# A 128-byte unused tile ahead of the constants of a one-layer decoder kernel

## The chip, the cores and the metric

The kernel runs on one core of a Trainium2 chip. The metric is the time of one execution on the device in microseconds, as the median of several runs; lower is better.

## What is computed

One layer of a decoder trunk on x of 1024 rows by 1024 columns, all in float32:

```python
x = x + 0.5 * swiglu(rms_norm(x, g_ffn1), w1_gate, w1_up, w1_down)      # D_FF = 2816
h = rms_norm(x, g_mix)
proj = h @ w_in                                                         # queries, keys, values, gates
y_a = dsa_attention(...)             # indexer, top 256 keys of each row, softmax, 8 heads
y_b = stick_breaking_attention(...)  # strictly causal, no softmax, 8 heads
merged = sigmoid(gate_a) * (y_a @ w_o_a) + sigmoid(gate_b) * (y_b @ w_o_b)
x = x + merged @ w_out
x = x + 0.5 * swiglu(rms_norm(x, g_ffn2), w2_gate, w2_up, w2_down)
```

## The kernel before

**Products.** A float32 operand is held as two halves, the part that fits TensorE's fast float32 form ("hi") and the rest ("lo"), and a product is three matmuls into one PSUM bank: hi by hi, hi by lo, lo by hi. `mm3` (L304 to L306) does this for the projections, `times` (L463 to L465) for the gate and up products of the two feed-forward blocks, and L672 to L674 for their down products. Both feed-forward blocks use Strassen's scheme: seven products of quarter matrices in place of eight, so sums and differences of quarters (S1 to S4 of the weights, T1 to T4 of the rows) are made first.

A matmul has a stationary operand (128 by 128, which the weight load puts into the array) and a moving one (here mostly 128 by 512, which streams through it). In float32 the moving one covers 2048 bytes of each partition and the stationary one 512 bytes.

```python
def times(a, b, ps, start=True):                                     # L460
    for k in range(4):
        c, l = slice(k * P, (k + 1) * P), slice(512 + k * P, 512 + (k + 1) * P)
        nc.tensor.matmul(ps, a[:, c], b[k][:, HI], ...)              # L463: a stationary, b moving
        nc.tensor.matmul(ps, a[:, c], b[k][:, LO], ...)              # L464
        nc.tensor.matmul(ps, a[:, l], b[k][:, HI], ...)              # L465
```

So a product of `times` is 12 matmuls. The products of one block stand in the order S1·T1 (bank pd), S2·T2 (pb), S3·T3 (pc), A12·B21 (pa), A22·T4 (pc), S4·B22 (pd), after A11·B11 (pa).

**Where tiles lie.** SBUF is handed out by pools from two ends. Pools of the left side stand behind the constants and small tiles, each behind the one opened before it; pools of the right side stand from the far end of SBUF downwards. The stationary operands of the feed-forward blocks come from `op`, which hands out tiles of two pools in turn:

```python
def ring(pool):                                                      # L737; NR = 5
    op = in_turn((wt, 4), (lambda name: pool.tile([P, 1024], F32R, tag="r", name=name, bufs=NR), NR))
```

`wt` is of the pool `outer` (right, 4 tiles), the other is `ring1` or `ring2` (left, 5 tiles), and `in_turn` (L308) takes them as right, left, right, left, right, left, right, left, left, and again. The moving operands of the gate and up products (B.., T..) lie in `t1` or `t2` (right); those of the down products come from `op` too.

**Places.** Nearly all tiles are a multiple of 512 bytes long, so a pool's tiles all begin at one place within 512 bytes. In the built program of the kernel before, tiles of left pools begin 352 bytes past a multiple of 512, and tiles of right pools 480 past one. "Place" below is this remainder; two tiles are "together" where it is the same, and "apart" where it is not. Exceptions are the small tiles and the weights of the index stage (tag `wM`, 4224 bytes, right side), whose places go on by 128 from tile to tile.

**Order.** In the feed-forward blocks the program's order is a schedule made at build time, in the attention stage one that the class `Weave` writes out from its own table of costs. Neither looks at addresses.

Of the kernel before, what the change touches and what calls it, by code (L numbers as in the profile page):

```python
# [10 lines left out]
F32 = mybir.dt.float32  # L11
# [12 lines left out]
P = 128  # L24
# [220 lines left out]
def trunk(ctx, tc, x, positions, g_ffn1, w1_gate, w1_up, w1_down, g_mix, w_in, g_cq, w_uq_a, w_q_idx,  # L245
          g_q_a, g_k_a, w_uv_a, w_o_a, w_o_b, w_out, g_ffn2, w2_gate, w2_up, w2_down, inv_freq, out):
    nc = tc.nc
    cst = ctx.enter_context(tc.tile_pool(name="cst", bufs=1))
# [16 lines left out]
        return small.tile([P, n], dt, name=name, bufs=bufs)  # L265


    ident = cst.tile([P, P], F32, name="ident")
    make_identity(nc, ident)
    mhalf = cst.tile([P, H], F32, name="mhalf")  # L270
# [1836 lines left out]
```

## Time and profile before

| | us |
|---|---|
| median of 3 runs | 2323.19 (2322.38 to 2325.25) |
| the profiled execution, own time | 2324.09 |
| its span from first to last instruction | 2322.3 |
| of that TensorE busy | 2211.2 (95%) |
| VectorE, ScalarE, GpSimd busy | 1590.9, 1114.3, 881.6 |

The stages in time: up to 342 us gate and up products of the first block with their opening, to 690 its down products, to 760 the first projections, to 1506 attention with the rest of the projections woven in, to 1640 the output projections, to 1980 the second block's gate and up products, to the end its down products (the lines run over these bounds a little). Matmuls follow each other faster than one takes from start to end, so what a matmul costs is read from one start to the next, not from its duration.

### The profile page before, as it was taken

To read this page: it belongs to the slowest core of one execution; us is meant where nothing else is said; L and a number is where in the kernel's file an instruction comes from. 1 tells how busy PE (TensorE), PEld (TensorE's weight loads), DVE (VectorE), ACT (ScalarE), POOL (GpSimd) and SP (SyncE) were. 2 spreads that over 40 slices of the span, in tenths; PEclk is the share of its full clock that TensorE was granted. 3 is DMA by queue.
4 is the path that set the end of the run, shared out by engine and by line. 5 is a ranking of instruction groups with operands and counts; after the bars stand their busy time and mean duration, and the time that the engine had idled before them with its cause. 6 is when DMAs were issued, how large, how long until landed. Compare 5 with 4: busy or idle time off the path is not lost.

```text
span 2322.3 us, 30186 instructions
## 1 busy us (share of the span) xinstructions
PE 2211.2 (95%) x10460; PEld 1811.4 (78%) x10460; DVE 1590.9 (69%) x2512; ACT 1114.3 (48%) x2133; POOL 881.6 (38%) x648
## 2 busy tenths in 40 slices
PE   7999999999999898889999699999999999999999
PEld 6788888878879777667788578877878888888877
DVE  5765656678862897666698877862476565667685
ACT  4323232334452479889988456633342323233443
POOL 3555555432252444211122133146245555542233
PEclk9999999999999999999999799999999999999999
DMA  5232323587664243645454533357313333358755
GB/s 165 75 114 91 114 87 116 159 307 241 168 208 116 81 132 98 163 98 128 109 138 120 172 109 97 128 178 254 118 59 109 96 107 98 105 163 291 234 168 181
DMA packets 252538, 330.64 MB, mean 142 GB/s; under 512 B 20577, under 2 KB 155377, under 8 KB 252385
## 3 DMA queue, kind: packets, MB, share of 16 engines
q1 hardware_dynamic: 235264, 288.83, 41.4%
q0 software_dynamic: 7488, 24.16, 2.7%
q10 hardware_dynamic: 9632, 15.73, 2.0%
q8 instruction: 82, 1.34, 0.2%
q14 instruction: 72, 0.58, 0.1%
HBM read 234.78 MB, written 93.88 MB: 142 GB/s over the span
## 4 chain that ended last, share of the span: by engine, by line
PE 70%; DVE 11%; ACT 9%; DMA 4%; issue 4%; POOL 1%; ACTq 0%; SPq 0%; DVEq 0%; POOLq 0%
PE p L673 5%; PE p L674 5%; PE p L672 5%; ACT junka L1127 4%; PE pc L463 3%; PE pc L465 3%; PE pc L464 3%; PE pd L465 3%; PE pd L463 3%; PE pd L464 3%; PE pa L463 3%; PE pa L465 3%; PE pa L464 3%; PE pb L463 2%; PE pb L465 2%
## 5 line engine op out<-in xcount | busy, mean ns | idle before, releaser
L1127 ACT ACTIVATE junka<-u,cand,sig 128x1024 bf16<-128x1024 f32 (+5 forms) x186 | 182.7, 982 | 22.1 <-DVE cand L1124 10.0
L1563 DVE TENSOR_TENSOR_SCAN left<-left 128x640 f32<-128x640 f32 (+3 forms) x64 | 92.7, 1449 | 3.8 <-ACT left L1555 3.8
L1612 DVE TENSOR_TENSOR pt<-pstT,pt 128x512 fp32r<-128x512 f32 (+1 forms) x96 | 51.3, 551 | 22.0 <-ACT pt L1610 21.4
L1664 PE MATMUL pstT<-ident,sa 128*128 128x128 f32 x288 | 47.4, 279 | 13.7 <-DVE pt L1612 12.0
L1729 DVE CUSTOM_DVE_ANT_0 e<-psL,bias 128x512 f32<-128x512 f32 (+3 forms) x96 | 49.4, 549 | 14.4 <-PE psL L1766 14.4
L1612 DVE TENSOR_TENSOR pt<-pspT,pt 128x512 fp32r<-128x512 f32 x72 | 46.5, 683 | 18.2 <-ACT pt L1610 18.2
L1741 ACT ACTIVATE e<-e,nm 128x256 f32<-128x256 f32 (+7 forms) x64 | 49.4, 774 | 18.5 <-DVE nm L1736 17.3
L1820 PE MATMUL pspT<-ident,e 128*128 128x128 f32 x288 | 42.0, 285 | 16.2 <-DVE ri L1743 9.2
L1566 DVE TENSOR_TENSOR sa<-sa,left 128x639 f32<-128x639 f32 (+3 forms) x64 | 53.1, 829 | 5.0 <-ACT sa L1557 1.8
L1664 PEld LDWEIGHTS pstT<-ident,sa 128*128 128x128 f32 x288 | 35.1, 142 | 26.2 <-DVE pt L1612 17.5
L673 PE MATMUL p<-bT,bS 128*128 128x512 f32 x132 | 51.8, 392 | 2.7 <-DVE bT L374 2.7
L1631 POOL DMA_DIRECT2D ybld<-yl x16 | 8.8, 551 | 118.8 <-DVE yl L1629 66.3
L1610 ACT ACTIVATE pt<-pspT 128x512 fp32r<-128x512 f32 x72 | 39.5, 596 | 29.8 <-PE pspT L1820 29.5
L673 PE MATMUL p<-aT,aS 128*128 128x512 f32 x132 | 51.8, 393 | 1.1 <-DVE aT L374 1.1
L1820 PEld LDWEIGHTS pspT<-ident,e 128*128 128x128 f32 x288 | 35.3, 146 | 22.5 <-DVE e L1744 9.5
L674 PE MATMUL p<-bT,bS 128*128 128x512 f32 x132 | 51.5, 393 | 0.8 <-POOL bS L374 0.8
L1610 ACT ACTIVATE pt<-pstT 128x512 fp32r<-128x512 f32 (+1 forms) x96 | 46.7, 501 | 11.6 <-PE pstT L1664 10.0
L1476 DVE SCALAR_TENSOR_TENSOR u<-relu,WI,u 128x512 f32<-128x512 f32 (+1 forms) x70 | 49.5, 727 | 3.9 <-ACT relu L1469 2.7
L674 PE MATMUL p<-aT,aS 128*128 128x512 f32 x132 | 50.9, 393 | 0.0
L1557 ACT ACTIVATE sa<-psz 128x512 f32<-128x512 f32 (+2 forms) x96 | 47.0, 503 | 5.0 <-ACT evg L1060 2.4
L1555 ACT ACTIVATE left<-psz 128x512 f32<-128x512 f32 (+2 forms) x96 | 45.4, 497 | 8.4 <-PE psz L1590 3.0
L1469 ACT ACTIVATE relu<-psdot 128x512 f32<-128x512 f32 (+1 forms) x80 | 40.0, 521 | 16.5 <-DVE u L1476 10.6
(3061 smaller groups left out, 8315.3 us busy)
## 6 DMA issues: line engine op xcount, KB each, us to landing
aw<-in_w_down_dram SPq DMA_DIRECT2D x33, 512.0 KB, 4.6
bw<-in_w_down_dram SPq DMA_DIRECT2D x33, 512.0 KB, 4.5
a0r<-in_w_gate_dram SPq DMA_DIRECT2D x22, 512.0 KB, 4.2
a1r<-in_w_up_dram SPq DMA_DIRECT2D x22, 512.0 KB, 4.7
b0r<-in_w_gate_dram SPq DMA_DIRECT2D x22, 512.0 KB, 4.1
b1r<-in_w_up_dram SPq DMA_DIRECT2D x22, 512.0 KB, 4.9
x<-in_x_dram SPq DMA_DIRECT2D x16, 512.0 KB, 6.5
gd<-evg ACTq DMA_DIRECT2D x32, 256.0 KB, 2.9
```

The costliest lines, as they stand in the source:

```text
L463: nc.tensor.matmul(ps, a[:, c], b[k][:, HI], start=start and k == 0, stop=False, skip_group_check=True)
L464: nc.tensor.matmul(ps, a[:, c], b[k][:, LO], start=False, stop=False, skip_group_check=True)
L465: nc.tensor.matmul(ps, a[:, l], b[k][:, HI], start=False, stop=k == 3, skip_group_check=True)
L672: nc.tensor.matmul(ps[q][m], S[:, h], T[:, HI], start=p == 0, stop=False)
L673: nc.tensor.matmul(ps[q][m], S[:, h], T[:, LO], start=False, stop=False)
L674: nc.tensor.matmul(ps[q][m], S[:, l], T[:, HI], start=False, stop=p == last)
L1127: nc.scalar.activation(junks[1][:, 0:(i + 1) * P], score[i], AF.Sign, scale=sig[:, b:b + 1], bias=cand.bitcast(F32)[:, b:b + 1], accum_out ...
L1563: nc.vector.tensor_tensor_scan(back, back, back, 1.0, op0=ALU.mult, op1=ALU.bypass)
L1610: nc.scalar.activation(pt[:, off:512], tp[:, off:512], AF.Copy)
L1612: nc.vector.tensor_sub(pt[:, 512 + off:1024], tp[:, off:512], f32(pt[:, off:512]))
L1664: nc.tensor.transpose(tp[:, q * P:(q + 1) * P], A[n + q][:, j * P:(j + 1) * P], ident)
L1820: nc.tensor.transpose(tp[:, q * P:(q + 1) * P], E[n + q][:, j * P:(j + 1) * P], ident)
```

## The change

```diff
@@ -265,6 +265,8 @@
         return small.tile([P, n], dt, name=name, bufs=bufs)
 
 
+
+    cst.tile([P, 32], F32, name="edge")
     ident = cst.tile([P, P], F32, name="ident")
     make_identity(nc, ident)
```

A tile of 128 bytes a partition is taken from the pool of constants, ahead of its first tile, and never used. The two built programs have the same 19,500 instructions in the same order on every engine, with the same waits; lines of the source move by two. What differs is addresses: every tile of a left pool lies 128 bytes higher (the identity `ident` at 16640 in place of 16512), and no tile of a right pool or of PSUM moves. Left tiles then begin 480 past a multiple of 512, as right ones do.

Of the 8,195 matmuls whose moving operand has 512 columns, 3,289 have the next matmul's stationary operand apart from their moving one before the change, and 72 after it. By lines these 3,289 are 2,100 of L463 to L465, 669 of L672 to L674, 378 of L304 to L306 and 142 of the attention stage's lines; 185 of the 378 stand between 1506 and 1640 us. The 72 that stay are among the 378.

## Rows read from the trace of the kernel before

**Rows 1.** From the page: busy time of each engine, and the chain of work that ended last, by engine and by line.

```profile
PE 2211.2 (95%) x10460; PEld 1811.4 (78%) x10460; DVE 1590.9 (69%) x2512; ACT 1114.3 (48%) x2133; POOL 881.6 (38%) x648
...
PE 70%; DVE 11%; ACT 9%; DMA 4%; issue 4%; POOL 1%; ACTq 0%; SPq 0%; DVEq 0%; POOLq 0%
PE p L673 5%; PE p L674 5%; PE p L672 5%; ACT junka L1127 4%; PE pc L463 3%; PE pc L465 3%; PE pc L464 3%; PE pd L465 3%; PE pd L463 3%; PE pd L464 3%; PE pa L463 3%; PE pa L465 3%; PE pa L464 3%; PE pb L463 2%; PE pb L465 2%
```

**Rows 2.** The chain of work that ended last, by line, in the stretch from 85 to 342 us.

```profile
by line: PE pd L465 9.3%; PE pc L463 9.3%; PE pd L463 9.3%; PE pd L464 9.2%; PE pc L464 9.2%; PE pc L465 9.1%; PE pa L463 8.7%; PE pa L465 8.6%; PE pa L464 8.6%; PE pb L463 4.7%; PE pb L464 4.7%; PE pb L465 4.7%; issue 0.7%; DVE as L584 0.7
```

**Rows 3.** Busy time of each engine by stage: stretch, its length, then busy us and instructions of each engine, granted clock as a share, DMA share, GB/s.

```profile
core 0: us, PE busy (x) PEld busy (x) DVE busy (x) ACT busy (x) POOL busy (x), PEclk, DMA share, GB/s
21.00:85.00 64.00, 62.95 (x323) 52.34 (x322) 45.81 (x62) 30.65 (x56) 24.69 (x18) 1.00 0.23 60
85.00:342.00 257.00, 255.21 (x1105) 207.40 (x1104) 162.59 (x176) 77.99 (x134) 136.50 (x96) 1.00 0.33 103
342.00:690.00 348.00, 344.70 (x1511) 280.03 (x1510) 253.93 (x338) 140.37 (x244) 133.97 (x89) 1.00 0.62 196
690.00:760.00 70.00, 67.39 (x544) 67.04 (x543) 21.27 (x56) 23.01 (x61) 24.73 (x33) 0.95 0.45 133
760.00:1506.00 746.00, 674.49 (x3426) 545.87 (x3425) 586.60 (x1250) 550.76 (x1148) 193.09 (x165) 0.97 0.44 121
1506.00:1640.00 134.00, 127.27 (x577) 104.69 (x577) 62.73 (x87) 45.26 (x65) 71.89 (x42) 0.97 0.64 214
1640.00:1705.00 65.00, 65.00 (x325) 54.24 (x324) 33.40 (x50) 22.99 (x42) 13.93 (x13) 1.00 0.18 57
1705.00:1980.00 275.00, 272.43 (x1187) 221.63 (x1187) 179.49 (x192) 87.20 (x150) 151.30 (x104) 1.00 0.32 101
1980.00:2322.00 342.00, 334.63 (x1449) 271.84 (x1448) 234.15 (x288) 125.37 (x220) 126.10 (x80) 1.00 0.59 192
```

**Rows 4.** Timeline of TensorE in the first block's gate and up products: start in us, duration, line, operation, out<-moving,stationary. The first matmul of each product (left out: its other matmuls); the last row is one that the schedule took later from the product that begins at 132.88.

```profile
121.83 0.39 PE L463 MATMUL pd<-aT,a02S 128*128 128x512 f32 x1
...
124.56 0.40 PE L463 MATMUL pb<-aT,a02S 128*128 128x512 f32 x1
...
127.35 0.39 PE L463 MATMUL pc<-aT,a02S 128*128 128x512 f32 x1
...
130.15 0.39 PE L463 MATMUL pa<-aB,a02A 128*128 128x512 f32 x1
...
132.88 0.40 PE L463 MATMUL pa<-aB,a12A 128*128 128x512 f32 x1
...
135.45 0.39 PE L463 MATMUL pc<-aT,a02A 128*128 128x512 f32 x1
...
138.24 0.40 PE L463 MATMUL pd<-aB,a02S 128*128 128x512 f32 x1
...
141.02 0.40 PE L465 MATMUL pa<-aB,a12A 128*128 128x512 f32 x1
```

**Rows 5.** The same view in the first block's down products, two stretches.

```profile
505.24 0.40 PE L672 MATMUL p<-aT,aA 128*128 128x512 f32 x1
...
507.99 0.40 PE L672 MATMUL p<-aT,aS 128*128 128x512 f32 x1
...
510.78 0.40 PE L672 MATMUL p<-aT,aA 128*128 128x512 f32 x1
...
513.58 0.62 PE L672 MATMUL p<-aT,aA 128*128 128x512 f32 x2
...
519.10 0.39 PE L672 MATMUL p<-aT,aS 128*128 128x512 f32 x1
...
521.82 0.40 PE L672 MATMUL p<-aT,aA 128*128 128x512 f32 x1
...
524.61 0.86 PE L672 MATMUL p<-aT,aS 128*128 128x512 f32 x3
...
527.38 0.39 PE L672 MATMUL p<-aT,aA 128*128 128x512 f32 x1
...
530.11 0.39 PE L672 MATMUL p<-aT,aS 128*128 128x512 f32 x1
```

**Rows 6.** The same view in the index stage: the first matmul of six with the index queries' weights (`wqi`) and the next matmul behind the six; then the first and the last of six with the queries' weights (`wuq`).

```profile
823.56 0.39 PE L304 MATMUL psq<-wqih,cqh 128*128 128x512 f32 x1
...
824.92 0.39 PE L1499 MATMUL psdot<-kih,qsi 128*128 128x512 f32 x1
...
876.37 0.39 PE L304 MATMUL psq<-wuqh,cqh 128*128 128x512 f32 x1
...
877.53 0.39 PE L306 MATMUL psq<-wuqh,cql 128*128 128x512 f32 x1
```

**Rows 7.** Timeline of GpSimd in the first block: four subtractions of `halve` (L374), with their durations.

```profile
106.17 1.29 POOL L374 TENSOR_TENSOR a02S<-a02s,a02S 128x512 fp32r<-128x512 f32 x1 [0.70 <-ACT a02S L373]
108.06 1.30 POOL L374 TENSOR_TENSOR a02S<-a02s,a02S 128x512 fp32r<-128x512 f32 x1 [0.60 <-ACT a02S L373]
109.31 1.29 POOL L374 TENSOR_TENSOR a02A<-a0r,a02A 128x512 fp32r<-128x512 f32 x1
111.62 1.30 POOL L374 TENSOR_TENSOR a02A<-a0r,a02A 128x512 fp32r<-128x512 f32 x1 [1.02 <-DVE a1u L484]
```

**Rows 8.** Timeline of TensorE: two sets of 16 transposes by the identity, each with its start, its duration in all and the count.

```profile
40.31 1.91 PE L423 MATMUL pst<-ident,x 128*128 128x128 f32 x16
...
50.42 1.91 PE L423 MATMUL pst<-ident,ay 128*128 128x128 f32 x16
```

**Rows 9.** Stretch of the whole span, busy us and instructions of TensorE and of its weight loads, of line L463 alone (L464 and L465 have as many).

```profile
0.00:2322.00 2322.00, 492.43 (x1248) 234.62 (x1248) 0.99 0.46 142
```

**Rows 10.** The same of line L672 alone (L673 and L674 have as many).

```profile
0.00:2322.00 2322.00, 227.12 (x616) 115.81 (x616) 0.99 0.46 142
```

**Rows 11.** Waits of TensorE in the feed-forward blocks: who waited for whom, us in total, times, longest.

```profile
PE p L673 <- DVE bT L374: 2.7, 1, 2.7
...
PE pc L463 <- DVE a0u L484: 1.8, 1, 1.8
...
PE pc L463 <- DVE b0u L484: 1.7, 1, 1.7
...
PE p L673 <- DVE aT L374: 1.1, 2, 0.8
```

**Rows 12.** Busy time by engine in the first 21 us (columns as in Rows 3).

```profile
0.00:21.00 21.00, 7.08 (x30) 6.32 (x31) 10.88 (x19) 10.66 (x18) 5.42 (x12) 1.00 0.98 308
```

## The prediction

> **What bounds the kernel now.** First the page's busy times and its chain. TensorE is busy 95% of the span and 70% of the chain is TensorE's own matmuls; VectorE comes next at 69% busy [rows 1]. An average over stages hides where that holds, so next the table by stage. In the two feed-forward blocks TensorE is idle for 1 to 7 us of a stage (255.21 of 257, 344.70 of 348, 65.00 of 65, 272.43 of 275, 334.63 of 342 with the tail), while VectorE is busy 162.59 of 257 and 253.93 of 348, and the transfers' share is 0.33 and 0.62 [rows 3]. The chain of one such stage consists of matmuls, with 0.7% for the largest other entry [rows 2]. In the attention stage it is otherwise: 674.49 of 746 for TensorE, 586.60 for VectorE and 550.76 for ScalarE [rows 3]. So a nanosecond on each matmul reaches the end in the feed-forward blocks and the output projections, and about half of it elsewhere. The granted clock is 1.00 in the feed-forward blocks [rows 3], the 2.4 GHz level, so the pace below is not the throttle's.
>
> The change moves no instruction, adds no wait and takes none. The only question is whether the place of a tile within 512 bytes has a price. The kernel answers it itself, since `op` gives its tiles in turn from both sides, and so half of its products have their two operands together and half apart. I read the timeline from the first matmul of a product to the first of the next and divide by the matmuls in between.
>
> In the gate and up products the moving operand is on the right (place 480) [rows 4]. With the stationary tile also on the right: 121.83 to 124.56 is 2.73 us for 12, 227.5 ns each; 130.15 to 132.88, 227.5; 138.24 to 141.02, 231.7. With the stationary tile on the left (place 352): 124.56 to 127.35 gives 232.5; 127.35 to 130.15, 233.3; 132.88 to 135.45 for 11 matmuls, 233.6; 135.45 to 138.24, 232.5. Means: 228.9 together, 233.0 apart, **4.1 ns** between them.
>
> In the down products both operands move about, which separates "same place" from "right side" [rows 5]. Both left: 505.24 to 507.99, 229.2; 519.10 to 521.82, 226.7; 527.38 to 530.11, 227.5. Both right: 524.61 to 527.38, 230.8. Moving right and stationary left: 507.99 to 510.78, 232.5, and 521.82 to 524.61, 232.5. Moving left and stationary right: 510.78 to 513.58, 233.3. Means: 228.6 together, 232.8 apart, **4.2 ns**. Neither side is slow; the mixed pairs are, both ways round.
>
> **Weighed against a rule.** Those rows show one matmul made slower by where its other operand lies. The Trainium skill, page "SBUF — State Buffer", section "Who interferes with whom", says that TensorE has two independent read ports, for the moving operand and for weight loads, and that only the port pair of VectorE and GpSimd causes contention. By it the sum would be zero and the time 2324.1 us as profiled; rows 4 and 5 disagree with it by 4 ns a matmul, and the measurement decides.
>
> **The change part by part.**
>
> *The tile itself.* No instruction writes or reads it: 0 us.
>
> *Gate and up products.* L463 has 1,248 matmuls, so the three lines 3,744 [rows 9]. Five of `op`'s nine tiles are on the left, so about 2,080 are apart; counted in the built program 2,100, and none afterwards. 2,100 × 4.1 ns = **8.6 us**, all on the chain.
>
> *Down products.* 3 × 616 = 1,848 matmuls [rows 10], of which 669 are apart. 669 × 4.2 ns = **2.8 us**, on the chain.
>
> *Output projections, 1506 to 1640 us.* 185 × 4.1 ns = 0.8 us; TensorE is busy 127.27 of 134 there [rows 3], so I count all of it.
>
> *Projections and attention between 690 and 1506 us.* 3,217 − 2,100 − 669 − 185 = 263 matmuls, 1.1 us, of which I count half, **0.5 us**: the rest ends in waits for VectorE and ScalarE, whose load there I showed above.
>
> *Transposes.* The identity moves by 128 bytes, so transposes of left tiles keep their distance from it and transposes of right tiles change theirs to what left ones have. Sixteen of right tiles take 1.91 us and sixteen of left tiles 1.91 us [rows 8]: 0 us.
>
> *Other engines.* GpSimd's subtraction takes 1.29 us with its source left and its target right, 1.30 with both left, 1.29 with both right and 1.30 with both left again [rows 7]: 0 us. Should VectorE, ScalarE or GpSimd change by a few ns, the feed-forward blocks have the slack shown above.
>
> *Waits that come next.* TensorE arrives some 0.5% sooner at what others make for it. The named waits in the feed-forward blocks are 2.7 us or less each [rows 11]; they follow a matmul's own end (the last product's bank, then VectorE, then the halves), so they move along with it and don't grow.
>
> Sum: 8.6 + 2.8 + 0.8 + 0.5 = 12.7 us. Against the profiled execution's own 2324.09 us that makes 2311.4; the median of the runs stands 0.9 us lower. A few of the counted matmuls stand ahead of a wait, so I don't take all of the 0.9 off: **2311 us**.
>
> Bounds of the price: the slowest product together (231.7) against the fastest apart (232.5) leaves 0.8 ns, the fastest together (226.7) against the slowest apart (233.6) 6.9 ns [rows 4, 5]. Over the 2,954 matmuls of the first three terms these are 2.4 and 20.4 us, that is 2321.7 and 2303.7. I take 4.1 and 4.2 because they are means of several products in two stages that agree.
>
> **The rivals.**
>
> *Nothing changes (chance 0.08).* Nearly every pair that is apart also has its tiles in different pools on different sides, far from each other; if that sets the 4 ns, moving one side by 128 bytes does nothing, and the time is 2324.1 as profiled. Against it stands the index stage, where all four tiles are on the right: six matmuls whose operands lie 0 or 256 apart take 823.56 to 824.92, 226.7 each, and those whose operands lie 128 or 384 apart take 876.37 to 877.53 for five, 232.0 each [rows 6]. Same line, same side, same shape: the place decides. It is only six of each, hence the 0.08. The rule of the skill on the two ports gives this time too.
>
> *The gain turns into waits (chance 0.08).* In the feed-forward blocks VectorE, GpSimd or the loads may be nearer to TensorE's heels than their busy shares say (VectorE 253.93 of 348 in the down products [rows 3]). If half of the 11.4 us there is lost so, the time is 2324.1 − 12.7 + 5.7 = 2317.1. For it: waits for the halves made by VectorE exist [rows 11]. Against it: they are 7.3 us in both blocks, and the chain hardly leaves TensorE [rows 2].
>
> *Slower, by transfers (chance 0.03).* Left tiles also change their place for transfers, from 352 to 480 in 512. If loads into left tiles and stores from them take longer there, the price is on the chain's transfer part, 4% of 2322.3 us or 93 us [rows 1], largely the start, where the transfers' share is 0.98 for 21 us [rows 12]. With the gain intact this decides from 12.7 of 93, that is if transfers take 14% longer: at 20% longer it costs 18.6 us and the time is 2330.0. Against it: right tiles already begin at 480 and are loaded beside left ones throughout, and the feed-forward stages leave the transfers' share at 0.33 and 0.62 [rows 3]; only part of the 93 us is left tiles. The Trainium skill, page "DMA: Bandwidth & Descriptors", section "How a descriptor splits into AXI transactions", bears on it: a descriptor that doesn't begin at a multiple of 256 bytes pays for the bytes before it. By its beats an estimate for a piece of 512 bytes is 19 beats from place 352 and 23 from 480, 21% more, and for one of 4096 bytes 131 and 135. No row here shows such a difference.
>
> That the tile would be placed where it moves nothing is not open: in the built program all left pools stand 128 higher, and 72 matmuls stay apart.
>
> **How the numbers follow.** The forecast has 0.81, the rivals 0.08, 0.08 and 0.03. About 0.2%, 4.6 us, is what a measurement of this kernel can tell from no change. Faster by more than that (under 2318.5) are the forecast but for its slow end, where the price is under 1.9 ns, and most of the second rival: 0.86. Within it: the first rival and those slow ends, 0.11. Slower: 0.03. The range for 8 in 10 is 2306 to 2318: down to a price of 6 ns, and up so that the second rival is in and the first and third are out.
>
> **What would show it.** In the profile after, a product such as the one at 124.56 (bank pb, S2) should take 2.73 us or so and not 2.79, as those together do now; the stretch of the gate and up products should shrink by about 2.5 us in each block's 257 us and the whole first block (to 690 us) by 5 to 6; TensorE's busy time should fall by some 13 us with the instructions unchanged; GpSimd's subtractions stay at 1.29 to 1.30. It is wrong if all products stay at 232 to 233 (first rival), if products reach 227 but the idle time between them grows (second), or if the first matmul starts later than now and the loads land late (third).

## The result, and the profile after

The changed kernel takes **2304.23 us** (median of 4 runs, 2299.10 to 2307.11) against 2323.34 in 4 runs of the kernel before: ratio **0.9914**, 95% interval 0.9896 to 0.9933, a gain of 19 us. The forecast said 2311.0 and 2306 to 2318: the sign is right, and the gain is half as large again as the 12 us named. The profiled execution took 2303.95 us, its span is 2302.2, 20.1 less than before.

From the page after, busy time of each engine and the chain by engine, which answer to [rows 1]:

```profile
PE 2188.7 (95%) x10460; PEld 1809.3 (79%) x10460; DVE 1591.4 (69%) x2512; ACT 1112.0 (48%) x2133; POOL 883.9 (38%) x648
...
PE 68%; DVE 11%; ACT 9%; DMA 5%; issue 4%; POOL 1%; ACTq 1%; SPq 0%; DVEq 0%; POOLq 0%
```

TensorE is busy 22.5 us less, with the same 10,460 instructions; VectorE and ScalarE differ by 0.5 and 2.3 us, GpSimd by 2.3. TensorE has 68% of the chain in place of 70%. So the matmuls became shorter, and TensorE still bounds the kernel.

Three of the stretches of [rows 3], in the profile after, with the same bounds and columns:

```profile
85.00:342.00 257.00, 255.06 (x1125) 210.63 (x1124) 164.38 (x178) 78.98 (x136) 139.01 (x97) 1.00 0.34 104
342.00:690.00 348.00, 344.88 (x1574) 285.83 (x1573) 259.40 (x349) 143.96 (x255) 140.60 (x96) 1.00 0.64 202
...
1705.00:1980.00 275.00, 273.13 (x1206) 225.92 (x1205) 180.77 (x194) 83.16 (x143) 150.69 (x104) 1.00 0.34 106
```

TensorE is as full as before in each (255.06 against 255.21 us, 344.88 against 344.70, 273.13 against 272.43), but more instructions fit in: 1125 for 1105, 1574 for 1511, 1206 for 1187. Per instruction the gate and up stretch went from 255.21/1105 = 231.0 ns to 255.06/1125 = 226.7.

How much of it reaches the end is read from the same matmuls in both traces, one execution of each kernel. Timeline of TensorE before, four matmuls: the last product of the first block's down products, one at the start of the output projections and one at their end, and one of the second block's down products near the end (start in us, duration; the rows' times are rounded to 0.01 us):

```profile
678.27 0.39 PE L674 MATMUL p<-aB,aA 128*128 128x512 f32 x1
...
1520.90 0.39 PE L305 MATMUL psoa<-yal,oa4h 128*128 128x512 f32 x1
...
1640.10 0.40 PE L305 MATMUL psout<-wout112l,m 128*128 128x512 f32 x1
...
2315.77 0.40 PE L674 MATMUL p<-bB,bA 128*128 128x512 f32 x1
```

The same four matmuls after (lines are two higher):

```profile
667.88 0.39 PE L676 MATMUL p<-aB,aA 128*128 128x512 f32 x1
...
1511.86 0.39 PE L307 MATMUL psoa<-yal,oa4h 128*128 128x512 f32 x1
...
1628.10 0.39 PE L307 MATMUL psout<-wout112l,m 128*128 128x512 f32 x1
...
2295.63 0.39 PE L676 MATMUL p<-bB,bA 128*128 128x512 f32 x1
```

The first block delivers 10.4 us by 678 us. At 1520.90 it is 9.0: in between, single gaps between TensorE's matmuls are up to 3.0 us longer or 1.5 us shorter than before, and two executions don't show whether the 1.4 us are lost to the change or to chance. At the end of the output projections it is 12.0, part of it by the granted clock, 0.97 of that stretch before [rows 3] and 0.99 after. The second block delivers the last 8.1 us, less than the first: at 2231 TensorE waits about 2.7 us for a tile in both traces, and behind that wait, in the trace after alone, eight matmuls run at the 1.2 GHz level, 427 ns from start to start (granted clock 0.97 in the 50 us from 2230); they cost some 1.7 us. In all 20.1 us arrive.

The products that answer to [rows 4] and [rows 5], in the profile after, first in the gate and up products, then in the down products (a first matmul of each):

```profile
120.53 0.39 PE L465 MATMUL pd<-aT,a02S 128*128 128x512 f32 x1
...
123.25 0.39 PE L465 MATMUL pb<-aT,a02S 128*128 128x512 f32 x1
...
125.97 0.39 PE L465 MATMUL pc<-aT,a02S 128*128 128x512 f32 x1
...
128.69 0.39 PE L465 MATMUL pa<-aB,a02A 128*128 128x512 f32 x1
...
510.64 0.39 PE L674 MATMUL p<-aT,aS 128*128 128x512 f32 x1
...
513.37 0.39 PE L674 MATMUL p<-aT,aA 128*128 128x512 f32 x1
```

S1 to S2 in bank pd, then pb, then pc: 2.72 us each, 226.7 ns a matmul, whichever side the stationary tile is on, where rows 4 showed 227.5, 232.5 and 233.3. The down product, from 510.64 to 513.37, takes 2.73. GpSimd's four subtractions of [rows 7] take 1.28 to 1.30 us.

What the prediction missed is seen inside one product that was *together* before. Timeline of TensorE before: two of the last matmuls of a product that is apart (bank pc, from 135.45), then matmuls of the product together behind it, which starts at 138.24 [rows 4]:

```profile
137.76 0.40 PE L464 MATMUL pc<-aT,a02A 128*128 128x512 f32 x1
138.00 0.40 PE L465 MATMUL pc<-aT,a02A 128*128 128x512 f32 x1
...
138.48 0.40 PE L464 MATMUL pd<-aB,a02S 128*128 128x512 f32 x1
...
140.10 0.39 PE L465 MATMUL pd<-aB,a02S 128*128 128x512 f32 x1
...
140.78 0.40 PE L465 MATMUL pd<-aB,a02S 128*128 128x512 f32 x1
```

The eight matmuls from 138.24 to 140.10 take 232.5 ns each, as slow as those of the product apart; the trace's own nanoseconds give the ninth 231, and 227 and 226 only to the tenth and the eleventh. The same product after:

```profile
136.62 0.39 PE L465 MATMUL pd<-aB,a02S 128*128 128x512 f32 x1
...
138.44 0.39 PE L467 MATMUL pd<-aB,a02S 128*128 128x512 f32 x1
...
139.34 0.39 PE L467 MATMUL pa<-aB,a12A 128*128 128x512 f32 x1
```

The same eight, from 136.62 to 138.44, take 1.82 us in place of 1.86, and the whole product, to 139.34, takes 2.72 in place of 2.78. So matmuls that are apart hand their slowness on to those behind them.

Each matmul with 512 columns, and another such matmul behind it, was paired with itself in the other trace (ns from its start to the next start, those without a wait between them), and grouped by what it was before. "Apart" is counted by the next matmul's stationary tile, as for the 3,289:

```
before the change                        count   before    after   saved
gate/up, apart                            2082   232.66   226.80   12.2 us
gate/up, together, within 12 of an apart  1368   229.09   226.72    3.2
gate/up, together, further behind          259   227.5    227.0     0.1
down, apart                                653   232.68   226.99    3.7
down, together, within 12                 1077   228.40   226.86    1.7
other stages, apart                        368   231.37   228.41    1.1
other stages, together, within 12          826   229.41   228.70    0.6
```

Together that is 22.6 us, of which 20.1 reached the end; those further behind in the down products (78) and in other stages (905) save nothing. By the distance behind the last apart matmul the mean before falls from 230.9 ns for the first to 227.2 for the tenth, and is 226.7 to 227.1 beyond. Of the 5.0 us that the matmuls together save in the feed-forward blocks, 1.0 belong to 158 that are the last of a product apart: their own stationary tile is apart, only the next one's is not.

### The profile page after: what moved, and what is told of

Same layout as the page of the kernel before. It is cut to its first block, busy times and chain, and to the rows that moved or that the text cites. A ratio compares the mean times of both kernels' runs of the same rounds, so it can differ in the third digit from the quotient of the medians.

```text
span 2302.2 us, 30186 instructions
## 1 busy us (share of the span) xinstructions
PE 2188.7 (95%) x10460; PEld 1809.3 (79%) x10460; DVE 1591.4 (69%) x2512; ACT 1112.0 (48%) x2133; POOL 883.9 (38%) x648
## 4 chain that ended last, share of the span: by engine, by line
PE 68%; DVE 11%; ACT 9%; DMA 5%; issue 4%; POOL 1%; ACTq 1%; SPq 0%; DVEq 0%; POOLq 0%
PE p L675 5%; PE p L676 5%; PE p L674 5%; ACT junka L1129 4%; PE pc L465 3%; PE pc L466 3%; PE pc L467 3%; PE pd L467 3%; PE pd L465 3%; PE pd L466 3%; PE pa L465 3%; PE pa L466 3%; PE pa L467 3%; PE pb L465 2%; PE pb L466 2%
```

## Experiments

Three theories. **A**: a matmul pays when TensorE's own two operands, the moving tile and the stationary tile that is loaded beside it, lie apart. **B**: part of the gain comes from other engines, whose tiles the change also moved against TensorE's. **C**: the sides or the pools count, not the place.

### The two halves of the change, apart

`e_ring_only` moves the ring tiles (the stationary operands) by 128 bytes and leaves all other left tiles at 352; `e_rest_only` moves all other left tiles and leaves the rings at 352. Neither touches an instruction.

```diff
 # e_ring_only; each pad moves what its pool hands out behind it
 def ring(pool):
+    pool.tile([P, 32], F32, name="ringpad", bufs=1)      # 128 bytes
...
+    spool.tile([P, 96], F32, name="pad1", bufs=1)        # the pools behind: 384 bytes, so back to 352
 # and the same with pad2, pad3 in the pools m0 and s2
 # e_rest_only: the change's own tile, then 96 in ring() and 32 in the three others
```

> Only the rings of the feed-forward blocks' stationary operands are moved by 128 bytes, to place 480; all other left tiles stay at 352. 515 of the wide matmuls stay apart, nearly all of them between 690 and 1640 us. Theory A: the feed-forward blocks gain as much as with the whole change, 18 us in all, so about 2305 us. Theory B: the matmuls that were together before gain nothing, since the other engines' tiles are where they were: 2,769 matmuls at 4.1 to 4.2 ns, 11.5 us, about 2312 us. Theory C: 2323 us.

> The reverse: all left tiles are moved by 128 bytes but for those of the rings, which stay at 352. 3,018 wide matmuls stay apart, those of the down products and the gate and up products as before. Theory A: gain only in the projections and attention, 1 to 2 us, 2321 to 2323 us. Theory B: the matmuls together gain 1.4 ns each, 4,900 of them, 7 us, about 2316 us.

Measured: `e_ring_only` 2306.21 us (2304.16 to 2311.88, 6 runs), ratio 0.9939 (0.9925 to 0.9954) against 2320.51 for the kernel before beside it; `e_rest_only` 2321.10 (2316.39 to 2326.06, 12 runs), ratio 0.9999 (0.9989 to 1.0009). TensorE is busy 2192.4 us in the first, near the 2188.7 of the full change, and 2206.0 in the second. Timeline of TensorE in `e_ring_only`, products pb, pc and pa of [rows 4]:

```profile
122.73 0.39 PE L463 MATMUL pb<-aT,a02S 128*128 128x512 f32 x1
...
125.45 0.39 PE L463 MATMUL pc<-aT,a02S 128*128 128x512 f32 x1
...
128.17 0.39 PE L463 MATMUL pa<-aB,a02A 128*128 128x512 f32 x1
```

and in `e_rest_only`, the same (lines one higher):

```profile
124.84 0.40 PE L464 MATMUL pb<-aT,a02S 128*128 128x512 f32 x1
...
127.63 0.39 PE L464 MATMUL pc<-aT,a02S 128*128 128x512 f32 x1
...
130.43 0.39 PE L464 MATMUL pa<-aB,a02A 128*128 128x512 f32 x1
```

2.72 and 2.72 us in the first, 2.79 and 2.80 in the second. The gain of `e_ring_only`, 14.3 us by the medians and 11 to 17 by the interval, lies between what A (18) and B (11.5) give, so the times alone don't decide between them. The matmuls do. Paired as in the table above, those of the feed-forward blocks that were together (within 12 of an apart one) take 226.7 ns in the gate and up products and 226.8 in the down products of `e_ring_only`, where the other engines' tiles are as before, and 229.0 and 228.3 in `e_rest_only`, where these tiles are moved; before they took 229.1 and 228.4. The matmuls of the feed-forward blocks save 21.1 us in the first, as with the full change (21.0), and 0.3 in the second; of the 515 matmuls that stay apart in the first, all but 12 stand in other stages. So the ring tiles carry the whole gain of the feed-forward blocks; moving the tiles that the other engines read and write, and many that transfers fill, is worth nothing that can be measured.

### TensorE alone

`m_pairs` (264.52 us in all) computes nothing of the reference. Its matmuls have the shapes and the order of `times`, but nothing else runs: four products with the stationary tile so many bytes past the moving one's place (`far`), then four together (`near`). In the `busy` parts all products are together, and ScalarE, VectorE and GpSimd work beside them on tiles at a distance.

```diff
+for off in (128, 384, 256, 64, 32, 448):
+    for n in range(4): product(off, f"far{off}x")       # stat[:, off/4 + ...], move[k]
+    for n in range(4): product(0, f"near{off}x")
+for off in (0, 128, 256, 384):                          # off: place of the other engines' tiles
+    for n in range(8): product(0, f"busy{off}x"); ...   # with 3 copies, 3 sums or subtractions, 1 on GpSimd
```

> A kernel of its own that computes nothing of the reference: products of 12 matmuls (128 by 128 stationary, 128 by 512 moving), TensorE alone, four products with the stationary operand 128, 384, 256, 64, 32, 448 bytes of 512 away from the moving one's place, each behind and ahead of four products with both together; then 8 products each, all together, while ScalarE, VectorE and GpSimd work on tiles 0, 128, 256, 384 bytes away from TensorE's place. Theory A (pairs of TensorE's own operands, and the slowness is handed on): together 226 to 227 ns from start to start, 128 and 384 away 232 to 233, 256 away 227; the first 5 to 10 matmuls together behind an apart product still take 228 to 236, then 227; the busy engines make no difference by their place (under 0.5 ns). Theory B (other engines' places): together 227 at once behind an apart product, and with busy engines 128 or 384 away 228.5 to 229 against 227 at 0. Theory C (the two sides of SBUF and not the place): no difference between any of the distances, since all tiles here lie in one pool.

Timeline of TensorE in `m_pairs`: the first matmul of each part (48 matmuls to the next; 96 in the `busy` parts):

```profile
22.53 0.40 PE L102 MATMUL far128x<-move,stat 128*128 128x512 f32 x1
...
33.69 0.39 PE L102 MATMUL near128x<-move,stat 128*128 128x512 f32 x1
...
44.58 0.40 PE L102 MATMUL far384x<-move,stat 128*128 128x512 f32 x1
...
55.73 0.39 PE L102 MATMUL near384x<-move,stat 128*128 128x512 f32 x1
...
66.62 0.39 PE L102 MATMUL far256x<-move,stat 128*128 128x512 f32 x1
...
77.50 0.39 PE L102 MATMUL near256x<-move,stat 128*128 128x512 f32 x1
...
88.38 0.40 PE L102 MATMUL far64x<-move,stat 128*128 128x512 f32 x1
...
99.58 0.39 PE L102 MATMUL near64x<-move,stat 128*128 128x512 f32 x1
...
132.57 0.39 PE L102 MATMUL far448x<-move,stat 128*128 128x512 f32 x1
...
143.56 0.39 PE L102 MATMUL near448x<-move,stat 128*128 128x512 f32 x1
...
154.44 0.39 PE L102 MATMUL busy0x<-move,stat 128*128 128x512 f32 x1
...
176.20 0.39 PE L102 MATMUL busy128x<-move,stat 128*128 128x512 f32 x1
...
197.96 0.39 PE L102 MATMUL busy256x<-move,stat 128*128 128x512 f32 x1
```

Divided by 48: 128 bytes away 232.5 ns, 384 away 232.3, 256 away 226.7, 64 away 233.3, 448 away 229.0; 32 away 233.3 as well. (The rows' rounding is worth 0.2 ns here: by the trace's own nanoseconds 128 and 384 are alike, 232.4.) Together 226.7 to 226.9, but 227.3 behind the part at 64. The first three `busy` parts take 21.76 us for 96, 226.7 each, with VectorE busy 18 to 21.5 us of it; the fourth, at 384, has 226.7 too. So the price needs no other engine, no transfer and no other side: B and C fall, A stands. The run also gives the floor, the time of a matmul without the price: 226.7, and with it a price of 5.8 ns at 128 and at 384. The rule that the prediction weighed (the Trainium skill, page "SBUF — State Buffer", section "Who interferes with whom") has TensorE's two read ports independent; this run does not agree, with 5.8 ns between places and only TensorE at work.

### How long the slowness lasts, and for which matmuls

`m_tails` (174.96 us), again TensorE alone and nothing of the reference: 3 matmuls together, then 1 to 11 apart, then 21 together; and 24 matmuls of 256 columns, or of bfloat16, at four distances.

```diff
+for off in (128, 384):
+    for n in (1, 2, 3, 4, 5, 6, 8, 11):
+        chain(f"tail{off}n{n}x", [0] * 3 + [off] * n + [0] * 21)
+for off in (0, 128, 64, 256): chain(f"half{off}x", [off] * 24, 256)          # 256 columns
+for off in (0, 128, 64, 256): chain(f"wide{off}x", [off] * 24, 512, True)    # bfloat16
```

> A kernel of its own that computes nothing of the reference, TensorE alone: in each bank 3 matmuls together, then 1, 2, 3, 4, 5, 6, 8 or 11 apart (128, then 384 bytes away), then 21 together; then 24 matmuls with 256 columns and 24 with 512 columns of bfloat16, at 0, 128, 64 and 256 bytes. Theory A (the slowness is handed on): behind some of the runs the matmuls together take 228 to 236 ns for up to 9 places, behind others they are at 226 to 227 at once, the same each time for the same run, since nothing else runs. If every one of them is at 226 to 227 from the second on, the slow matmuls together in the kernel before come from something else. With 256 columns no distance makes a difference of over 1 ns, as the kernel before showed (119 to 120 ns either way); for bfloat16 I have no row and expect the same classes as in float32, or none.

Timeline of TensorE in `m_tails`, some of its parts with their count (start, duration of the part):

```profile
21.44 5.84 PE L104 MATMUL tail128n1x<-move,stat 128*128 128x512 f32 x25
27.12 6.14 PE L104 MATMUL tail128n2x<-move,stat 128*128 128x512 f32 x26
33.10 6.33 PE L104 MATMUL tail128n3x<-move,stat 128*128 128x512 f32 x27
...
66.45 8.18 PE L104 MATMUL tail128n11x<-move,stat 128*128 128x512 f32 x35
74.46 5.84 PE L104 MATMUL tail384n1x<-move,stat 128*128 128x512 f32 x25
...
127.48 3.04 PE L104 MATMUL half0x<-move,stat 128*128 128x256 f32 x24
130.35 3.00 PE L104 MATMUL half128x<-move,stat 128*128 128x256 f32 x24
133.19 2.99 PE L104 MATMUL half64x<-move,stat 128*128 128x256 f32 x24
...
138.90 5.35 PE L104 MATMUL wide0x<-bmove,bstat 128*128 128x512 bf16 x24
144.09 5.34 PE L104 MATMUL wide128x<-bmove,bstat 128*128 128x512 bf16 x24
149.27 5.34 PE L104 MATMUL wide64x<-bmove,bstat 128*128 128x512 bf16 x24
```

From the start of one part to the next, less 226.7 ns for each matmul: with one apart 5.68 us for 25, 0.01 over; with two 5.98 us for 26, 0.08 over by the unrounded starts; with eleven 8.01 us for 35, 0.08 over. Matmul by matmul, the part with two reads 232 (the last one ahead of them), 241, 240 (the two), and then 235, 233, 236, 224, 231, 236, 228, 233, 231 for nine that are together, before it falls to 226 and 227; behind eleven only one is slow. So two apart matmuls cost far more than 6 ns each, and how long the slowness runs on depends on how many there were, without growing with them. The series at 384 is the same to 0.01 us. With 256 columns the apart ones are not slower but faster: 2.87 us for 24 together (119.6 ns), 2.84 apart (118.3). In bfloat16 with 512 columns it is 5.19 and 5.18 us, 216 ns, at both. Of the three forms only float32 with 512 columns, the one that fills this kernel, shows the price.

### Other distances in the kernel itself

Pads as in `e_ring_only`, with other sizes, and the other left tiles at 352 in each: the rings 256 bytes from the right tiles (`e_ring_256`, pads of 384 and 128 bytes), 64 below them (`e_ring_m64`, 64 and 448) and 64 above them (`e_ring_p64`, 192 and 320).

```diff
-    pool.tile([P, 32], F32, name="ringpad", bufs=1)
+    pool.tile([P, 96], F32, name="ringpad", bufs=1)      # e_ring_256; 16 in e_ring_m64, 48 in e_ring_p64
```

> The rings are moved by 384 bytes, to place 224, which is 256 away from the right tiles at 480; all else stays. If what counts is the place within 256 bytes (as six matmuls of the index stage hinted), the time is that of the rings at 480: about 2305 us by theory A, 2312 by B. If what counts is the place within 512 bytes, 2,895 matmuls are still apart and the time is 2321 to 2325 us.

Measured 2304.05 us (2299.32 to 2311.85, 4 runs), ratio 0.9932 (0.9913 to 0.9951), TensorE busy 2188.3 us. The full change has 0.9914 (0.9896 to 0.9933) and 2188.7, and the feed-forward matmuls save 21.2 us here against 21.0. So the place within 256 bytes is what counts, as in `m_pairs`; the prediction's "place of a tile within 512 bytes" asks for more than is needed.

> The rings lie at place 416, 64 bytes below the right tiles at 480; all else as before the change. From the pairs measured by themselves (448 of 512 away: 228.7 ns and no slow matmuls behind; 64 away: 233.3 and seven slow ones behind): the 2,100 of the gate and up products gain 3.9 ns each and what they hand on, 8.3 + 3.2 us; of the down products half gain 3.9 ns and half lose 0.7, 1.1 us: about 12.5 us faster than before, 2308 to 2310 us. If only equal places (or 256) help, the time is that of before, 2320 to 2323 us.

Measured 2312.43 us (2308.31 to 2320.97, 5 runs), ratio 0.9949 (0.9931 to 0.9967) against 2322.36 beside it. Timeline of its TensorE, products pb and pc:

```profile
124.55 0.39 PE L463 MATMUL pb<-aT,a02S 128*128 128x512 f32 x1
...
127.30 0.39 PE L463 MATMUL pc<-aT,a02S 128*128 128x512 f32 x1
```

The product pb takes 2.75 us, between 2.72 and 2.79. Over the trace the gate and up matmuls that are apart (448) take 228.86 ns, where 228.7 was expected. The down products, however, mix both ways: a moving tile on the right is 448 from a left stationary one (229.94), a moving one on the left 64 (232.18), and the matmuls together behind them take 229.4, more than the 228.4 before. They gained nothing, where 1.1 us were expected, and the matmuls together of the gate and up products gained 2.1 us in place of 3.2. So the feed-forward matmuls save 10.0 us of the 12.5 expected; the interval of the time (8 to 16 us) holds both.

> The rings lie at place 32, which is 64 bytes above the right tiles at 480 (512 and over); all else as before. By the same pairs the 2,100 matmuls of the gate and up products cost 0.7 ns more than at 128 away, 1.5 us, and hand on slowness over seven matmuls, some 2 to 3 us more, and half of the down products gain 1.3 us: 2 to 4 us slower than before, 2323 to 2327 us. If the sign of the distance does not count, the time is that of the rings at 416.

Measured 2323.58 us (2317.04 to 2329.32, 10 runs), ratio 1.0012 (0.9997 to 1.0027). The gate and up matmuls that are apart take 233.04 ns, as 64 does in `m_pairs`, and those together behind them 229.0, no more than before, so the 2 to 3 us that were to be handed on didn't come. The interval holds no change as well as a loss of 2 to 4 us, as expected. The two kernels have the same distance of 64 bytes between the sides, with opposite signs, and lie 11 us apart: the distance has a sign.

## Why the prediction was right, and where its size failed

*That the place has a price, and that it is TensorE's own.* Right, shown by `e_rest_only` (nothing) and `m_pairs` (the price without any other engine). The six matmuls of the index stage [rows 6] were good evidence: `m_pairs` gives 226.7 and 232.4 for the same distances. The rival that nothing changes falls with it.

*Which matmuls count.* Right: 2,100, 669, and a few hundred in other stages. Means of all apart matmuls before were 232.66 and 232.68, where the prediction read 233.0 and 232.8 from a handful.

*The price, 4.1 and 4.2 ns: the step that failed.* The prediction took it as the distance between two means ("228.9 together, 233.0 apart, **4.1 ns** between them"). But of the products together those at 138.24 (231.7), 524.61 (230.8) and 505.24 (229.2) were themselves slowed by what stood ahead of them, and the last matmul pays as well where the next product's stationary tile lies apart from it (at 140.78 it takes 233 ns). Against the floor the price is 232.66 − 226.80 = 5.9 ns in the gate and up products and 232.68 − 226.99 = 5.7 in the down products. On the counted matmuls that is 12.2 + 3.7 = 15.9 us in place of 8.6 + 2.8 = 11.4.

*The gain of matmuls that were together: a term put at nothing.* Counted as zero, it is 3.2 + 0.1 + 1.7 = 5.0 us in the feed-forward blocks. The same error, met twice: the reference was taken among rows that the effect itself had touched. The spread of the products together, 226.7 to 231.7 [rows 4, 5], was the sign of it, and lay in the prediction as a bound of the price (6.9 ns) rather than as a question. The range ended at a price of 6.0 with nothing gained by the together ones, and so at 2306.

*Output projections, projections and attention.* 0.8 + 0.5 us named, 1.1 + 0.6 saved there by TensorE's matmuls. The first block was to be 5 to 6 us shorter at its end, and was 10.4 at 678.27.

*Waits that come next.* Nearly right: 22.6 us saved, 20.1 arrive. In the feed-forward stretches shown TensorE stays as full as before, and the rival by which half of that gain turns into waits falls. What is missing is lost between 678.27 and 1520.90 (1.4 us) and in the second block's down products, there mostly by the eight matmuls at the lower clock, and partly made up in the output projections. One execution of each doesn't show whether the change has a part in that.

*Transfers, transposes, GpSimd.* Nothing: `e_rest_only`, where the other left tiles start at 480, is not slower, and GpSimd's subtractions stay at 1.28 to 1.30 us.

What stays open is whether a matmul's own stationary tile counts, or only the next one's. The next one's does: in the trace before, 50 matmuls whose own tiles are together, with at least thirteen together ahead of them, and whose next one's stationary tile is apart take 232.1 ns, and 622 in the same position with the next one's together take 227.0; in `m_tails` the matmul ahead of a single apart one takes 232 as well. That one takes 234 itself, but there the slowness handed on would do as much, and no run separates the two. Open too: why the slowness runs on, and for how long; why 448 costs 2.3 ns and 64 6.6.

## What to carry to other kernels

Where float32 matmuls of 512 columns fill the time (in the fast form that this kernel uses), let stationary and moving tiles begin at the same place within 256 bytes, and count every tile, pad or constant that shifts a pool by another amount; it costs no instruction. When a price is read as a difference within one trace, take the floor from instances far behind any disturbed one, and ask why the undisturbed group spreads before averaging it. A kernel with the disputed pair alone, a few tens of products long, gives price and floor in one profile.

## What the runs showed of the hardware that was not expected

- Matmuls that are together run slow behind ones that are apart, nine of them behind two: two apart matmuls cost 0.08 us in all, as much as eleven, and one costs 0.01.
- A matmul whose own two tiles are together is slowed by the next one's stationary tile: 232.1 ns against 227.0.
- The distance has a sign: 64 bytes past the moving tile's place 233.3 ns, 64 short of it (448) 229.0, with 226.7 at 0 and 256.
- At 256 columns 128 bytes apart is 1.3 ns faster (118.3 against 119.6), and bfloat16 shows no difference (216 ns).
